# Token-major projections in a one-core hybrid attention block

## The chip, the core and the metric

The kernel runs on one core of a Trainium2 chip. The metric is device time: 1773.85 us, the median of 3 runs (1772.23 to 1774.06). TensorE multiplies, ScalarE (ACT) and VectorE (DVE) move, cast and combine, GpSimd (POOL) does a few side jobs, and SyncE (SP) issues nearly all transfers.

## The reference

One decoder block over 256 tokens of 2048 features, in float32, with weights of some 400 MB that are each read once.

```python
h = rmsnorm(x, norm_mix_g) * (1.0 + scale_m) + shift_m     # shift, scale, gate: silu(c) @ ada_w + ada_b
(p_q, p_k, p_v, p_g, p_gk, p_cq, p_ckv, p_kr, p_ga, p_gb) = split(h @ w_in)
o = gla_chunked(q, k, v, log_a)                            # gated linear attention, 4 heads
y_gla = (rmsnorm(o, gla_onorm_g) * silu(p_g)) @ gla_wo
y_mla = mla_attention(q_nope, q_rope, k_nope, k_rope, v_m) @ mla_wo      # 16 heads, causal softmax
merged = sigmoid(p_ga) * y_gla + sigmoid(p_gb) * y_mla
x = x + gate_m * (merged @ w_out)
h = rmsnorm(x, norm_ffn_g) * (1.0 + scale_f) + shift_f
g, u = split(h @ ffn_w_in)                                 # 2 x 5632 columns
x = x + gate_f * ((silu(g) * u) @ ffn_w_down)
out = rmsnorm(x, final_norm_g)
```

## The kernel before

Every product is made of three matmuls in the format fp32r. A weight piece `raw` of two k-tiles (2 x 128 rows) by 512 columns, 512 KB, is loaded by SyncE; ScalarE casts it to `hi` (L107), VectorE makes `lo = raw - hi` (L108), and TensorE adds hi x hi, hi x lo and lo x hi into PSUM. Such a piece is a *half* below, a *k-tile* is 128 of its rows. There are 6 raw buffers (up to 10 where spare slots are lent) and 3 each of `hi` and `lo`.

A group is 512 output columns over all 16 k-tiles and takes two PSUM banks (`mm`). It comes in two forms. `form_a` (L160) keeps a block of 128 tokens stationary and streams 512 weight columns: 6 matmuls for a k-tile, and the result lies token-major, 128 tokens by 512 features for each t. `form_b` (L170) keeps 128 weight columns stationary and streams 256 tokens: 12 matmuls for a k-tile, and the result lies feature-major, which is the form that a following projection needs as its activations.

The stages, in order: first projections of h in four rounds over its rows (jobs "a" and "b"; five of the eight branch gate groups are jobs 11 to 15), the low-rank attention (MLA) two heads at a time with the other three gate groups (`gate_stream`) and the linear attention's scores (GLA) between, GLA's output gate (`full(form_a, w_in, O_G ...)`), `mla_wo` gated, `gla_wo` with the merge, `w_out` with the residual, then the FFN: 11 chunks of a g group and a u group, and the down projection, whose 8 accumulators (2 token blocks by 4) take all PSUM banks.

The order of work: `tick()` runs after each half and moves what lies in the background, by paces (`pace`): the conditioning products (`ada_steps`), which load further 512 KB pieces and use VectorE, and two lanes of generators (`ATT`, two at a time, and `GLA`, one at a time); each `yield` there is a wait for the next tick. A scheduler then sets each engine's order by its own model of time.

In `mla_wo` and `gla_wo` the gates, which the first stages left in DRAM, come back as `mg` and `gaT` (`gate_in`, with the sigmoid); the group's PSUM result is multiplied by it, the two branches are added, and `mh`, `ml` are the merged tile's hi and lo for `w_out`. In the FFN, `sg` is silu of g, and the product of u and `sg` goes to `acts`; chunks 2 to 9 also turn two blocks of `x1` (the residual) over for the end, by four transposes (L884). A transpose is a TensorE matmul with an identity into an `aux` bank (2 of these), copied out by ScalarE.

Of the kernel before, what the change touches and what calls it, by code (L numbers as in the profile page):

```python
# [9 lines left out]
F32 = mybir.dt.float32  # L10
# [8 lines left out]
S = 256  # L19
P = 128  # L20
# [31 lines left out]
def tile_block(ctx: ExitStack, tc: tile.TileContext, x, positions, ada_w, ada_b, w_in, gla_gk_w, gla_wo,  # L52
# [18 lines left out]
    def k256(t):  # L71
        return t.rearrange("p (k t) -> p k t", t=S)
# [9 lines left out]

# [1 line left out]
    turn = [0]  # L84
# [95 lines left out]
    def group(form, w, c0, ah, al, nk, cols=512):  # L180
        ps = [mm_bank(), mm_bank()]
        for k in range(0, nk, 2):
            form(ps, half(w, k, c0, cols), ah, al, k, k == 0, k + 2 == nk, cols)
            yield ps
# [33 lines left out]

# [1 line left out]
    vec = const.tile([P, 164], F32, name="vec")  # L220
# [18 lines left out]

# [1 line left out]
    mod = const.tile([P, 96], F32, name="mod")  # L241
# [82 lines left out]

# [1 line left out]
    x_sp = dram.tile([P, 4096], F32, name="x_sp")  # L326
# [15 lines left out]

# [1 line left out]
    sin_t = const.tile([P, S], F32, name="sin_t")  # L344
# [31 lines left out]

# [1 line left out]
    latv = qk = vtv = None  # L378
# [30 lines left out]
    jobs += [("a", O_V + 512 * i, 512, vtv[:, :, 512 * i:512 * (i + 1)], None) for i in range(4)]  # L409
    jobs += [("b", o + 512 * i, 512, d, None) for (o, i), d in zip(gates, gdst)]  # L410
    NJ, PIN = len(jobs), 3
# [14 lines left out]
    for r in range(4):  # L426
# [38 lines left out]
        if r == 0:  # L465
# [3 lines left out]
            ang, ang2 = rope_angles()  # L469
# [1 line left out]
            pgk = const.tile([GR, S], F32, name="pgk")  # L471
# [3 lines left out]
            def latents():  # L475
# [10 lines left out]
                rsqrt_mean(rl, ssq, QR, 4)  # L486
                # rotary key on both halves of the partitions
                krd = sb(512, "sc", 2)[:, 0:S]
# [49 lines left out]

# [1 line left out]
    om = slot(5)  # L540
# [46 lines left out]
    def gate_stream():  # L587
        for o, i in gates[5:]:
            for ps in group(form_b, w_in, o + 512 * i, hhk, hlk, KT):
                yield  # L590
            st = raw_tile()
            for j in range(2):
                A.copy(out=st[:, 512 * j:512 * (j + 1)], in_=ps[j])
            G.dma_start(out=spill[o][:, 1024 * i:1024 * (i + 1)], in_=st)
# [44 lines left out]
    def gla_att(h):  # L639
# [9 lines left out]
        yield  # L649
        # log decay, times 16  # L650
        ps = gx_bank()
# [68 lines left out]

# [1 line left out]
    gt = slot(4)  # L722
# [53 lines left out]

# [1 line left out]
    oml = slot(1, F32R)  # L778
# [15 lines left out]
    for i in range(4):  # L794
        for n, ps in enumerate(group(form_b, mla_wo, 512 * i, k256(omh), k256(oml), KT)):
            tick()
            gate_in(mg, gb_sp, i, n)
        for j in range(2):
            d = mg[:, 1024 * i + 512 * j:1024 * i + 512 * (j + 1)]
            V.tensor_tensor(out=d, in0=ps[j], in1=d, op=ALU.mult)  # L800
    assert not GLA.busy()
    gaT = slot(3)
# [1 line left out]
    pace[0] = 0.65  # L804
    mh, ml = slot(2, F32R), slot(1, F32R)
    for i in range(4):
        for n, ps in enumerate(group(form_b, gla_wo, 512 * i, oghk, oglk, KT)):
            tick()
            gate_in(gaT, ga_sp, i, n)
        for j in range(2):  # L810
            cs = slice(1024 * i + 512 * j, 1024 * i + 512 * (j + 1))
            V.tensor_tensor(out=gaT[:, cs], in0=ps[j], in1=gaT[:, cs], op=ALU.mult)
            V.tensor_tensor(out=mg[:, cs], in0=mg[:, cs], in1=gaT[:, cs], op=ALU.add)
            A.copy(out=mh[:, cs], in_=mg[:, cs])
            V.tensor_tensor(out=ml[:, cs], in0=mg[:, cs], in1=mh[:, cs].bitcast(F32), op=ALU.subtract)

# [1 line left out]
    hold[0] = True  # L818
# [3 lines left out]
    for i in range(4):  # L822
# [7 lines left out]
        for j in range(4):  # L830
            k = 4 * i + j
            V.scalar_tensor_tensor(out=x1k[:, k], in0=ps[j // 2][:, (j % 2) * S:(j % 2 + 1) * S],
                                   scalar=mod[:, 32 + k:33 + k], in1=x1k[:, k], op0=ALU.mult, op1=ALU.add)
# [1 line left out]
    acc = sb(512, "w0")[:, :S]  # L835
# [29 lines left out]
    pace[0] = 0.5  # L865
    for ch in range(FFN // 512):
        if ch == 1:
            bg.append(slow())
        ps = full(form_b, ffn_w_in, 512 * ch, k256(fh), k256(fl), KT)
        sg = [sb(512, "w2"), sb(512, "w3")]  # L870
        for j in range(2):
            A.activation(out=sg[j], in_=ps[j], func=AF.Silu)
        ps = full(form_b, ffn_w_in, FFN + 512 * ch, k256(fh), k256(fl), KT)
        if ch == 8:
            acts[2] = slot(1)
        a = acts[ch // 4][:, (ch % 4) * 1024:(ch % 4 + 1) * 1024]
        for j in range(2):
            V.tensor_tensor(out=a[:, 512 * j:512 * (j + 1)], in0=ps[j], in1=sg[j], op=ALU.mult)
        if 2 <= ch < 10:
            k = 2 * (ch - 2)  # L880
            tp = aux_bank()
            for t in range(2):
                for kk in range(2):
                    T.transpose(out=tp[:, t * S + kk * P:t * S + (kk + 1) * P],  # L884
                                in_=x1k[:, k + kk, t * P:(t + 1) * P], identity=ident)
            A.copy(out=x1tv[:, :, k * P:(k + 2) * P], in_=tp.rearrange("p (t d) -> p t d", t=2))

    background(1000)
    acc = [[mm_bank() for _ in range(4)], [aux_bank(), aux_bank(), gx_bank(), gx_bank()]]
    NK, HELD = FFN // P, 4  # L890
# [7 lines left out]
    for k in range(NK):  # L898
# [10 lines left out]
        for hf in range(2):  # L909
            raw = load_raw(ffn_w_down[0, k * P:(k + 1) * P, hf * 1024:(hf + 1) * 1024], 1, 1024)  # L910
            if late:
                o = (k - NK + HELD) % 2 * 2048 + hf * 1024
                hi, lo = [u[:, o:o + 1024] for u in lh[(k - NK + HELD) // 2 * 2:][:2]]
                A.copy(out=hi, in_=raw[:, 0])
                V.tensor_tensor(out=lo, in0=raw[:, 0], in1=hi.bitcast(F32), op=ALU.subtract)
                ws.append((hi, lo))
                continue
            (hi, lo), = split_raw(raw, 1, 1024)
            for t in range(2):
                for n in range(2):  # L920
                    down(acc[t][2 * hf + n], ah, al, hi, lo, t, n, k == 0, False)
        if late:
            held.append((ah, al, ws))

# [1 line left out]
    ot = slot(4)  # L926
# [51 lines left out]
```

## Time and profile before

| | us |
|---|---|
| median of 3 runs | 1773.85 |
| span of the profiled execution | 1771.8 |
| TensorE busy | 1733.6 (98%) |
| VectorE busy | 1229.8 (69%) |
| ScalarE busy | 836.7 (47%) |
| DMA moved | 418.93 MB, mean 236 GB/s |

The profiled execution's own time is this span with what little lies around it; the runs' median is 2.05 us above the span. Busy times overlap between engines, and those of pipelined matmuls overlap among themselves, so the distance between two starts on TensorE tells more than a duration.

### The profile page before, as it was taken

To read this page: it belongs to the slowest core of one execution; us is meant where nothing else is said; L and a number is where in the kernel's file an instruction comes from. 1 tells how busy PE (TensorE), PEld (TensorE's weight loads), DVE (VectorE), ACT (ScalarE), POOL (GpSimd) and SP (SyncE) were. 2 spreads that over 40 slices of the span, in tenths; PEclk is the share of its full clock that TensorE was granted. 3 is DMA by queue.
4 is the path that set the end of the run, shared out by engine and by line. 5 is a ranking of instruction groups with operands and counts; after the bars stand their busy time and mean duration, and the time that the engine had idled before them with its cause. 6 is when DMAs were issued, how large, how long until landed. Compare 5 with 4: busy or idle time off the path is not lost. (4 is left out here: it accounts for less than half of the span.)

```text
span 1771.8 us, 31106 instructions
## 1 busy us (share of the span) xinstructions
PE 1733.6 (98%) x12416; PEld 1640.9 (93%) x12416; DVE 1229.8 (69%) x1764; ACT 836.7 (47%) x1278; POOL 96.9 (5%) x136
## 2 busy tenths in 40 slices
PE   6999999999999999999999999999999999999997
PEld 6899999899999988999999899999999999888885
DVE  7899887587777477888887856667564444455556
ACT  5544445356767655544444443333334333444443
POOL 1360000000000110000000000000000000000001
PEclk8999999999999999999999899999999999999999
DMA  9999886564445497999999567778775555555553
GB/s 359 322 325 303 283 308 216 181 204 150 152 136 178 134 329 253 350 356 329 332 321 305 203 201 257 244 227 267 234 226 181 182 185 179 179 191 191 191 189 106
DMA packets 207377, 418.93 MB, mean 236 GB/s; under 512 B 12960, under 2 KB 31840, under 8 KB 206592
## 3 DMA queue, kind: packets, MB, share of 16 engines
q1 hardware_dynamic: 205472, 410.39, 69.0%
q0 software_dynamic: 1616, 6.49, 1.0%
q8 instruction: 97, 1.59, 0.4%
q14 instruction: 48, 0.39, 0.1%
q10 hardware_dynamic: 144, 0.07, 0.0%
HBM read 408.51 MB, written 8.39 MB: 235 GB/s over the span
## 5 line engine op out<-in xcount | busy, mean ns | idle before, releaser
L108 DVE TENSOR_TENSOR lo<-raw,hi 128x1024 fp32r<-128x1024 f32 (+3 forms) x524 | 603.1, 1156 | 411.9 <-ACT hi L107 410.9
L176 PE MATMUL mm<-s,hi 128*128 128x256 f32 x3072 | 873.0, 285 | 2.5 <-ACT hi L107 2.1
L177 PE MATMUL mm<-s,hi 128*128 128x256 f32 x3072 | 869.2, 284 | 0.0
L178 PE MATMUL mm<-s,lo 128*128 128x256 f32 x3072 | 862.9, 284 | 2.0 <-DVE lo L108 2.0
L107 ACT CAST hi<-raw 128x1024 fp32r<-128x1024 f32 (+3 forms) x524 | 511.2, 982 | 676.7 <-PE mm L177 440.0
L176 PEld LDWEIGHTS mm<-s,hi 128*128 128x128 f32 x3072 | 590.5, 192 | 4.6 <-ACT hi L107 2.2
L177 PEld LDWEIGHTS mm<-s,hi 128*128 128x128 f32 x3072 | 590.8, 192 | 0.5 <-DVE s L781 0.2
L178 PEld LDWEIGHTS mm<-s,lo 128*128 128x128 f32 x3072 | 586.3, 192 | 3.6 <-DVE lo L108 2.7
L267 DVE SCALAR_TENSOR_TENSOR ada<-raw,cact,ada 128x512 f32<-128x512 f32 (+1 forms) x293 | 212.1, 728 | 7.9 <-DMA raw<-in_ada_w_dram 5.4
L107 ACT CAST hi<-s 128x1024 fp32r<-128x1024 f32 (+1 forms) x76 | 78.1, 1028 | 104.4 <-PE mm L177 62.2
L167 PE MATMUL mm<-lo,s 128*128 128x512 f32 (+1 forms) x320 | 123.9, 388 | 0.3 <-DVE lo L108 0.3
L168 PE MATMUL mm<-hi,s 128*128 128x512 f32 (+1 forms) x320 | 121.4, 382 | 1.7 <-DVE s L322 1.7
L166 PE MATMUL mm<-hi,s 128*128 128x512 f32 (+1 forms) x320 | 112.1, 386 | 0.9 <-ACT s L321 0.9
L108 DVE TENSOR_TENSOR lo<-s,hi 128x1024 fp32r<-128x1024 f32 (+1 forms) x76 | 91.4, 1203 | 29.7 <-ACT hi L107 29.4
L168 PEld LDWEIGHTS mm<-hi,s 128*128 128x128 f32 x320 | 60.7, 190 | 12.4 <-DVE s L322 2.0
L167 PEld LDWEIGHTS mm<-lo,s 128*128 128x128 f32 x320 | 60.7, 190 | 11.8 <-issue 0.8
L166 PEld LDWEIGHTS mm<-hi,s 128*128 128x128 f32 x320 | 60.2, 191 | 11.2 <-ACT s L321 1.2
L895 PE MATMUL mm<-lo,w 128*128 128x512 f32 x160 | 62.7, 392 | 0.0
L896 PE MATMUL mm<-hi,w 128*128 128x512 f32 x160 | 62.4, 392 | 0.0
L267 DVE SCALAR_TENSOR_TENSOR ada<-s,cact,ada 128x512 f32<-128x512 f32 (+1 forms) x79 | 57.7, 730 | 1.5 <-DMA s<-in_ada_w_dram 0.9
L894 PE MATMUL mm<-hi,w 128*128 128x512 f32 x160 | 50.4, 393 | 1.3 <-ACT w L902 1.3
L451 DVE TENSOR_TENSOR s<-mm,s 128x512 f32<-128x512 f32 (+1 forms) x62 | 40.5, 672 | 1.1 <-PE mm L178 0.7
(271 smaller groups left out, 1562.4 us busy)
## 6 DMA issues: line engine op xcount, KB each, us to landing
raw<-in_ffn_w_in_dram SPq DMA_DIRECT2D x176, 512.0 KB, 4.4
raw<-in_ada_w_dram SPq DMA_DIRECT2D x150, 512.0 KB, 5.0
raw<-in_w_in_dram SPq DMA_DIRECT2D x128, 512.0 KB, 4.6
raw<-in_ffn_w_down_dram SPq DMA_DIRECT2D x88, 512.0 KB, 4.5
s<-in_ada_w_dram SPq DMA_DIRECT2D x42, 512.0 KB, 5.8
s<-in_w_in_dram SPq DMA_DIRECT2D x32, 512.0 KB, 4.6
raw<-in_mla_wo_dram SPq DMA_DIRECT2D x20, 512.0 KB, 6.1
raw<-in_gla_wo_dram SPq DMA_DIRECT2D x20, 512.0 KB, 6.7
```

The lines of the kernel that those rows point to most:

```text
L107: A.copy(out=hh_, in_=rr)
L108: V.tensor_tensor(out=ll_, in0=rr, in1=hh_.bitcast(F32), op=ALU.subtract)
L166: T.matmul(ps[t][:, :cols], lhsT=ah[:, k, ts], rhs=hi, start=st, stop=False)
L167: T.matmul(ps[t][:, :cols], lhsT=ah[:, k, ts], rhs=lo, start=False, stop=False)
L168: T.matmul(ps[t][:, :cols], lhsT=al[:, k, ts], rhs=hi, start=False, stop=en)
L176: T.matmul(o, lhsT=hi[:, pick], rhs=ah[:, k], start=st, stop=False, skip_group_check=True)
L177: T.matmul(o, lhsT=hi[:, pick], rhs=al[:, k], start=False, stop=False, skip_group_check=True)
L178: T.matmul(o, lhsT=lo[:, pick], rhs=ah[:, k], start=False, stop=en, skip_group_check=True)
L267: ins = V.scalar_tensor_tensor(out=acc, in0=raw[:, k - k0], scalar=c, in1=acc, op0=ALU.mult, op1=ALU.add)
L894: T.matmul(o, lhsT=ah[:, ts], rhs=hi[:, ns], start=first, stop=False)
L895: T.matmul(o, lhsT=ah[:, ts], rhs=lo[:, ns], start=False, stop=False)
L896: T.matmul(o, lhsT=al[:, ts], rhs=hi[:, ns], start=False, stop=last)
```

## The change

Four projections go from `form_b` to `form_a`: the eight branch gate groups, `mla_wo`, `gla_wo` and the FFN's first projection. What lies in DRAM and in `mg` and `gaT` is then token-major, and so are the gating and the merge. Where the next projection wants features first, two generators in the lane `ATT` turn the result over: `turn_over` the merged tile (8 transposes for a group, then hi and lo from PSUM), `turn_act` the FFN's product (8 transposes for a chunk, then a copy to `acts`), both two ticks after the group. The `x1` transposes become a generator too (`turn_x1`). Before the down projection's first piece is done, the lane is emptied, and its second token block takes the `gx` banks first.

```diff
-    jobs += [("b", o + 512 * i, 512, d, None) for (o, i), d in zip(gates, gdst)]
+    jobs += [("a", o + 512 * i, 512, d.rearrange("p (t c) -> p t c", t=2), None) for (o, i), d in zip(gates, gdst)]
...
-            for ps in group(form_b, w_in, o + 512 * i, hhk, hlk, KT):
+            for ps in group(form_a, w_in, o + 512 * i, hhk, hlk, KT):
...
-        for n, ps in enumerate(group(form_b, mla_wo, 512 * i, k256(omh), k256(oml), KT)):
+        for n, ps in enumerate(group(form_a, mla_wo, 512 * i, k256(omh), k256(oml), KT)):
...
+    def turn_over(i):
+        yield
+        yield
+        for j in range(2):
+            ps = aux_bank()
+            for b in range(2):
+                for t in range(2):
+                    c0 = 1024 * i + 512 * t + (2 * j + b) * P
+                    T.transpose(out=ps[:, b * S + t * P:b * S + (t + 1) * P], in_=mg[:, c0:c0 + P], identity=ident)
+            cs = slice(1024 * i + 512 * j, 1024 * i + 512 * (j + 1))
+            A.copy(out=mh[:, cs], in_=ps)
+            V.tensor_tensor(out=ml[:, cs], in0=ps, in1=mh[:, cs].bitcast(F32), op=ALU.subtract)
+            yield
+
     for i in range(4):
-        for n, ps in enumerate(group(form_b, gla_wo, 512 * i, oghk, oglk, KT)):
+        for n, ps in enumerate(group(form_a, gla_wo, 512 * i, oghk, oglk, KT)):
...
-            A.copy(out=mh[:, cs], in_=mg[:, cs])
-            V.tensor_tensor(out=ml[:, cs], in0=mg[:, cs], in1=mh[:, cs].bitcast(F32), op=ALU.subtract)
+        ATT.wait.append(turn_over(i))
...
+    def turn_act(ch, sg):
+        yield
+        yield
         if ch == 8:
             acts[2] = slot(1)
         a = acts[ch // 4][:, (ch % 4) * 1024:(ch % 4 + 1) * 1024]
         for j in range(2):
-            V.tensor_tensor(out=a[:, 512 * j:512 * (j + 1)], in0=ps[j], in1=sg[j], op=ALU.mult)
+            tp = aux_bank()
+            for b in range(2):
+                for t in range(2):
+                    T.transpose(out=tp[:, b * S + t * P:b * S + (t + 1) * P],
+                                in_=sg[t][:, (2 * j + b) * P:(2 * j + b + 1) * P], identity=ident)
+            A.copy(out=a[:, 512 * j:512 * (j + 1)], in_=tp)
+            yield
...
-        ps = full(form_b, ffn_w_in, FFN + 512 * ch, k256(fh), k256(fl), KT)
+        ps = full(form_a, ffn_w_in, FFN + 512 * ch, k256(fh), k256(fl), KT)
+        for t in range(2):
+            V.tensor_tensor(out=sg[t], in0=ps[t], in1=sg[t], op=ALU.mult)
+        ATT.wait.append(turn_act(ch, sg))
         if 2 <= ch < 10:
...
+            ATT.wait.append(turn_x1(2 * (ch - 2)))
...
-    acc = [[mm_bank() for _ in range(4)], [aux_bank(), aux_bank(), gx_bank(), gx_bank()]]
+    acc = [[mm_bank() for _ in range(4)], [gx_bank(), gx_bank()]]
...
+            if k == 0 and hf == 1:
+                while ATT.busy():
+                    ATT.step()
+                acc[1] += [aux_bank(), aux_bank()]
```

How the instructions move is seen at three places. The first is TensorE in `gla_wo`, near the start of its second group; `s` is an activation tile (hi or lo part), `ada` a conditioning accumulator, the `s` of L815 the merged tile `mg`. Before:

```order
L176 MATMUL mm<-s_6934,hi 128x256
L177 MATMUL mm<-s_7617,hi 128x256
L178 MATMUL mm<-s_6934,lo 128x256
L176 MATMUL mm<-s_6934,hi 128x256
L289 MATMUL aux<-ident,ada 128x128 x4
L177 MATMUL mm<-s_7617,hi 128x256
```

And in the change:

```order
L166 MATMUL mm<-hi,s_5978 128x512
L167 MATMUL mm<-lo,s_5978 128x512
L168 MATMUL mm<-hi,s_5979 128x512
L166 MATMUL mm<-hi,s_5978 128x512 x2
L815 MATMUL aux<-ident,s_6859 128x128 x8
L167 MATMUL mm<-lo,s_5978 128x512
L168 MATMUL mm<-hi,s_5979 128x512
```

One matmul of 512 stands for two of 256, and the eight transposes of `turn_over` stand together, after 26 matmuls of the new group.

The second is VectorE at the end of `gla_wo`'s first group, where the products (L812, now L827), the sums (L813, now L828) and the lo parts (L815, now L818) are made. Before:

```order
L812 TENSOR_TENSOR s_8774<-mm,s_8774 128x512 x2
L267 SCALAR_TENSOR_TENSOR ada<-raw,cact,ada 128x512
L813 TENSOR_TENSOR s_7627<-s_7627,s_8774 128x512 x2
L108 TENSOR_TENSOR lo<-raw,hi 128x1024
L267 SCALAR_TENSOR_TENSOR ada<-raw,cact,ada 128x512
```

And in the change:

```order
L827 TENSOR_TENSOR s_7622<-mm,s_7622 128x512 x2
L267 SCALAR_TENSOR_TENSOR ada<-raw,cact,ada 128x512
L828 TENSOR_TENSOR s_6859<-s_6859,s_7622 128x512 x2
L108 TENSOR_TENSOR lo<-raw,hi 128x1024
L267 SCALAR_TENSOR_TENSOR ada<-raw,cact,ada 128x512
```

Products and sums stand as before; the lo parts move further back.

The third is TensorE where the FFN ends and the down projection begins; `w_16697` and `w_13207` are the hi and lo of its first activations, `w_13049` and `w_13050` the last chunk's products. Before:

```order
L178 MATMUL mm<-s_11034,lo 128x256
L176 MATMUL mm<-s_11034,hi 128x256
L177 MATMUL mm<-s_11035,hi 128x256
L178 MATMUL mm<-s_11034,lo 128x256
L894 MATMUL mm<-hi,w_16697 128x512
L895 MATMUL mm<-lo,w_16697 128x512
```

And in the change:

```order
L167 MATMUL mm<-lo,s_9538 128x512
L168 MATMUL mm<-hi,s_9539 128x512
L890 MATMUL aux<-ident,w_13049 128x128 x2
L890 MATMUL aux<-ident,w_13050 128x128
L890 MATMUL aux<-ident,w_13049 128x128
L890 MATMUL aux<-ident,w_13050 128x128 x2
L890 MATMUL aux<-ident,w_13049 128x128
L890 MATMUL aux<-ident,w_13050 128x128
L925 MATMUL mm<-hi,w_13207 128x512
```

The last chunk's eight transposes stand between, with no other matmul.

## Rows read from the trace of the kernel before

**Rows 1.** The page: busy time by engine; TensorE's granted clock in 40 slices.

```profile
PE 1733.6 (98%) x12416; PEld 1640.9 (93%) x12416; DVE 1229.8 (69%) x1764; ACT 836.7 (47%) x1278; POOL 96.9 (5%) x136
PEclk8999999999999999999999899999999999999999
```

**Rows 2.** TensorE's waits: engine, line, releaser, us in total, times, longest.

```profile
PE aux L213 <- DVE e L212: 4.0, 2, 3.0
...
PE mm L894 <- ACT w L902: 1.3, 1, 1.3
```

**Rows 3.** Groups by line and shape, TensorE: count, busy us, mean ns.

```profile
L176 PE MATMUL mm<-s,hi 128*128 128x256 f32 x3072 | 873.0, 285 | 2.5 <-ACT hi L107 2.1 <-ACT s L321 0.3
...
L166 PE MATMUL mm<-hi,s 128*128 128x512 f32 x256 | 92.3, 394 | 0.0
```

**Rows 4.** TensorE's timeline in the FFN: start us, duration us, line, tile, count.

```profile
1235.55 0.60 PE L884 MATMUL aux<-ident,s 128*128 128x128 f32 x4
1235.90 0.36 PE L176 MATMUL mm<-s,hi 128*128 128x256 f32 x1
1236.10 0.28 PE L177 MATMUL mm<-s,hi 128*128 128x256 f32 x1
...
1282.05 0.60 PE L884 MATMUL aux<-ident,s 128*128 128x128 f32 x4
```

**Rows 5.** TensorE's timeline in the output gate's projection, form a.

```profile
659.91 0.39 PE L166 MATMUL mm<-hi,s 128*128 128x512 f32 x1
660.14 0.39 PE L167 MATMUL mm<-lo,s 128*128 128x512 f32 x1
...
666.74 0.62 PE L166 MATMUL mm<-hi,s 128*128 128x512 f32 x2
```

**Rows 6.** ScalarE's timeline in the down projection: first and last of 32 casts.

```profile
1539.42 0.40 ACT L902 CAST w<-s 128x256 fp32r<-128x256 f32 x1
...
1710.30 0.40 ACT L902 CAST w<-s 128x256 fp32r<-128x256 f32 x1
```

**Rows 7.** TensorE's timeline at transposes between form a matmuls.

```profile
701.22 1.03 PE L751 MATMUL gx<-ident,s 128*128 128x128 f32 x8
702.00 0.48 PE L167 MATMUL mm<-lo,s 128*128 128x512 f32 x1
702.32 0.39 PE L168 MATMUL mm<-hi,s 128*128 128x512 f32 x1
```

**Rows 8.** Line L886, the copies from PSUM: ns min/median/max, first and last start.

```profile
L886 ACT COPY s<-aux x8: 567/579/587, 1003.0 to 1469.1; 128x512 f32<-128x512 f32 x8
```

**Rows 9.** VectorE's timeline at the end of `gla_wo`'s first group.

```profile
830.66 1.28 DVE L812 TENSOR_TENSOR s<-mm,s 128x512 f32<-128x512 f32 x2
...
832.52 1.28 DVE L813 TENSOR_TENSOR s<-s,s 128x512 f32<-128x512 f32 x2
```

**Rows 10.** Timeline of all engines where the down projection begins.

```profile
1514.04 1.46 DVE L878 TENSOR_TENSOR s<-mm,w 128x512 f32<-128x512 f32 x2
...
1514.49 0.28 PE L178 MATMUL mm<-s,lo 128*128 128x256 f32 x1
...
1515.65 0.71 ACT L902 CAST w<-s 128x256 fp32r<-128x256 f32 x2
...
1516.10 0.50 PE L894 MATMUL mm<-hi,w 128*128 128x512 f32 x1 [1.32 <-ACT w L902]
```

**Rows 11.** Stretches: us, busy PE, PEld, DVE, ACT, POOL, granted clock, DMA share, GB/s.

```profile
1003.00:1006.00 3.00, 2.89 (x13) 2.89 (x14) 2.96 (x8) 2.85 (x7) 0.00 (x0) 0.50 0.00 0
140.00:160.00 20.00, 20.00 (x167) 19.91 (x166) 20.00 (x33) 10.02 (x19) 0.00 (x0) 1.00 0.84 274
720.00:740.00 20.00, 19.96 (x167) 19.67 (x167) 16.35 (x23) 12.13 (x21) 2.29 (x12) 1.00 1.04 388
760.00:780.00 20.00, 20.00 (x169) 20.00 (x168) 17.23 (x22) 8.30 (x8) 0.00 (x0) 1.00 1.03 381
```

**Rows 12.** SyncE's waits between 700 and 800 us.

```profile
SPq L98 <- DVE lo L108: 44.7, 28, 4.1
```

More of the change, by code (lines that the diff above doesn't have):

```diff
@@ L865, in tile_block @@
     pace[0] = 0.5
[L866 to L872, printed above, removed]
-        ps = full(form_b, ffn_w_in, FFN + 512 * ch, k256(fh), k256(fl), KT)
+    def turn_act(ch, sg):
+        yield
+        yield
         if ch == 8:
@@ L877, in tile_block, with turn_x1 @@
         for j in range(2):
-            V.tensor_tensor(out=a[:, 512 * j:512 * (j + 1)], in0=ps[j], in1=sg[j], op=ALU.mult)
-        if 2 <= ch < 10:
[L880 to L886, printed above, removed]
+            tp = aux_bank()
[5 more added lines that the diff above has]
+            yield
+    def turn_x1(k):
+        tp = aux_bank()
+        for t in range(2):
+            for kk in range(2):
+                T.transpose(out=tp[:, t * S + kk * P:t * S + (kk + 1) * P],
+                            in_=x1k[:, k + kk, t * P:(t + 1) * P], identity=ident)
+        A.copy(out=x1tv[:, :, k * P:(k + 2) * P], in_=tp.rearrange("p (t d) -> p t d", t=2))
+        yield
+    assert not ATT.busy()
+    for ch in range(FFN // 512):
+        if ch == 1:
+            bg.append(slow())
+        ps = full(form_a, ffn_w_in, 512 * ch, k256(fh), k256(fl), KT)
+        sg = [sb(512, "w2"), sb(512, "w3")]
+        for t in range(2):
+            A.activation(out=sg[t], in_=ps[t], func=AF.Silu)
+        ps = full(form_a, ffn_w_in, FFN + 512 * ch, k256(fh), k256(fl), KT)
+        for t in range(2):
+            V.tensor_tensor(out=sg[t], in0=ps[t], in1=sg[t], op=ALU.mult)
+        ATT.wait.append(turn_act(ch, sg))
+        if 2 <= ch < 10:
+            ATT.wait.append(turn_x1(2 * (ch - 2)))
     background(1000)
-    acc = [[mm_bank() for _ in range(4)], [aux_bank(), aux_bank(), gx_bank(), gx_bank()]]
+    acc = [[mm_bank() for _ in range(4)], [gx_bank(), gx_bank()]]
     NK, HELD = FFN // P, 4
```

## The prediction

> **What bounds the kernel now.** I read the head of the page first: TensorE is busy for 98% of the span, and its granted clock is at the upper level (2.4 GHz) in every slice but the first, which shows 0.8 [rows 1]. A busy share of pipelined matmuls says little about how fast they go, so next come TensorE's own waits: after the first loads the longest are 4.0 us in two for `rows_of` (the row of inverse norms) and 1.3 us where the down projection starts [rows 2]. So TensorE's instruction stream is the bound: what counts is how far apart its instructions start, not how long one is under way (285 ns and 394 ns in the list by shape [rows 3], both mostly pipeline). The timeline gives the distances.
>
> Form b (a weight block stationary, 256 tokens moving): one chunk of the first FFN projection, from one set of four transposes to the next, takes 1282.05 - 1235.55 = 46.50 us for 2 groups x 16 k-tiles x 12 matmuls = 384 matmuls and the set [rows 4]. The set costs 1235.90 - 1235.55 = 0.35 us, and the first matmul behind it 0.20 instead of 0.12, together 0.43. (46.50 - 0.43) / 384 = 0.120 us per matmul of 256 columns.
>
> Form a (a token block stationary, 512 weight columns moving), in the output gate's projection: 30 matmuls from 659.91 to 666.74, so 6.83 / 30 = 0.2277 us [rows 5]. The down projection has the same shapes; there, 31 steps of 24 matmuls lie between two casts, (1710.30 - 1539.42) / 31 / 24 = 0.2297 us [rows 6]. Two matmuls of 256 take 0.240, one of 512 takes 0.228 to 0.230: each instruction carries some 13 ns besides its columns.
>
> **The change part by part.** *Matmuls.* 608 k-tiles of 512 output columns go from form b to form a: 80 in the first rounds (five gate jobs x 16), 48 in `gate_stream`, 64 in `mla_wo`, 64 in `gla_wo`, 352 in the FFN. Each removes 12 matmuls and adds 6. I take 0.228 per matmul: the new order has runs of three as in rows 5 and pairs of L166 as before the transposes, and rows 5 are the same code. 12 x 0.120 - 6 x 0.228 = 0.072 us; x 608 = 43.8 us saved. With rows 5 alone it is 0.074 and 44.8, with rows 6 0.062 and 37.6. TensorE has no cover here, so the time goes from the path unless something else becomes late.
>
> *Transposes.* 32 for the merged branches, 88 for the FFN's activations: 120. Among form a matmuls eight of them took 702.00 - 701.22 = 0.78 us, 0.0975 each, and the first matmul behind them 0.32 instead of 0.23, so 0.09 per set [rows 7]. The order cuts the 120 into 23 sets: 11.7 + 2.1 = 13.8 us. By rows 4 (0.43 per four) it would be 12.9; if each four stood alone by rows 7 (0.48) 14.4. The eight sets of `x1` transposes existed before; now they stand in 15 pieces (7 x 0.09 = 0.6), and two of the sets, which stood right behind `rows_of`, where TensorE waited 3.0 us at a time [rows 2], lose that cover (at most 8 x 0.11 = 0.9). Together 1.5.
>
> *Copies.* ScalarE gets 22 more copies from PSUM at about 0.58 us [rows 8], 12.8 us. ScalarE is busy for 47% of the span [rows 1]; these cost nothing unless a cast of `hi` is late for them, and in the FFN there are two such casts' worth of slack (three `hi` buffers). VectorE's operations stay the same in number and shape: the split of the merged tile reads PSUM now, the product reads the same.
>
> *The waits that are added.* Each set of transposes needs the finished product, and all that follows on TensorE queues behind it. In `gla_wo` the two products and the two sums end 832.52 + 1.28 - 830.66 = 3.1 us after the group [rows 9]; in the new order 26 matmuls, 5.9 us, stand between the group's end and the set. So these waits should be zero. At one place there is nothing between: where the FFN ends, eight transposes, a copy and a cast come in a chain before the first matmul of the down projection, because the cast writes the buffer that the transposes read. Before, that matmul came 1516.10 - 1514.49 = 1.61 us after the last one of the FFN, behind the second product (1514.04 + 1.46) and a cast [rows 10]. Now: products until about 1.9, transposes 0.87, copy 0.58, cast and start about 0.7, so 4.0: 2.4 more, of which 0.9 is in the transposes already. 1.5 us.
>
> The clock: after the 3.0 us wait before `rows_of` the granted clock stood at 0.50, the lower level, from 1003 to 1006 [rows 11]; after the 1.3 us wait at the down projection's start it did not fall [rows 1, 2]. The new waits there are about 2 us and then 1.2. If the clock falls, some 3 us at half speed cost 1.5 more.
>
> *What the faster stream runs into.* From 140 to 160 us VectorE is busy 20.00 of 20 us [rows 11]: in the first two rounds the conditioning work is level with TensorE, and I count the 15 halves of gate jobs there (30 k-tiles, 2.2 us) as not gained. In `mla_wo` the DMA engines are at a mean share of 1.03 to 1.04 with up to 388 GB/s [rows 11], yet SyncE mostly waits for buffers that VectorE has to free (44.7 us in that window [rows 12]), so transfers still run ahead; I count nothing there.
>
> Sum: -43.8 + 13.8 + 1.5 + 1.5 + 2.2 = -24.8 us. The profiled execution has a span of 1771.8 us, and the median of the runs is 2.05 above it, which I leave as it is: 1773.85 - 24.8 = 1749.
>
> The Trainium skill speaks against the change at this point. Its page "TensorE: Matmul & The Clock Gate" (section "Back-to-back issue gap") has an isolated gap of N / 2.4 + 2.5 ns at full clock, 109 ns for 256 columns and 216 for 512, so that what an instruction costs beyond its columns is small. By that a k-tile would save 0.016 us, 608 of them 9.5, and 120 transposes would cost 6.7 (56 ns each): an estimate of 2.8 us gained, too little to be seen. This case's rows 4 to 6 show 120 and 228 to 230 ns instead.
>
> **The rivals.** 0.2% of the time, 3.5 us, is about what a measurement of this kernel can tell from no change.
>
> *The cover ends: 1758.* The data or VectorE become the bound in `mla_wo` and `gla_wo`, whose 128 k-tiles (9.2 us) then gain nothing: 24.8 - 9.2 = 15.6. For it: the DMA share above 1 in rows 11. Against: rows 12, and that the `hi` and `lo` buffers let TensorE run two halves ahead.
>
> *The instruction's own cost isn't saved: 1774, no change.* If the converted stages ran at 0.235 us per matmul, each k-tile would save 0.030 us, 18 in all, just what the additions cost (13.8 + 1.5 + 1.5). Against: all form a rows lie at 0.2277 to 0.2297, with the same code. It is also where the rule of the Trainium skill would end.
>
> *TensorE waits at its own transposes: slower, 1785.* The place is the first set behind each group in `gla_wo` and the FFN, 14 of them (4 and 10). If VectorE finishes the product late, TensorE stands, since the set comes in order before the next group's matmuls. It decides against the change from (24.8 + 3.5) / 14 = 2.0 us of wait at each, that is products 7.9 us after the group's end; at 2.6 us it would be 1749 + 36 = 1785. For it: VectorE has `lo` and conditioning work queued between. Against: 3.1 us in rows 9, and an emptier VectorE in the FFN.
>
> **How the numbers follow.** My forecast, 1749, gets 0.76; the ended cover 0.16; no change 0.04; slower 0.04. The likeliest case's own range is 1742 (44.8 saved, 12.9 for the transposes, nothing lost at the rounds or the clock: 30 us, and 2 us for the spread of the runs) to 1757 (37.6 saved, 14.4 for the transposes, the clock's 1.5: 16.5). The range for 8 in 10 reaches into the ended cover: 1742 to 1760. Faster by over 0.2%: 0.92, within it 0.04, slower 0.04.
>
> **What would show it.** In the profile after: L166 to L168 at 0.228 apart through the FFN, and a chunk (2 x 96 matmuls with 8 or 12 transposes) in 44.7 to 45.3 us against 46.50. No TensorE wait at the transposes of L815 and L890 but at the last chunk, and about 4 us from the last FFN matmul to the first of L925. ACT and VectorE with the same busy time but for 12.8 us on ACT. I am wrong if L166 to L168 come at 0.235 or more, if `hi` waits for a DMA in `mla_wo`, or if the waits on VectorE before L815 and L890 sum to over 10 us.

## The result

The changed kernel takes 1747.92 us (median of 4 runs, 1746.09 to 1749.22) against 1773.45 (4 runs, 1772.23 to 1774.06): a ratio of 0.9855, 95% interval 0.9841 to 0.9869. The profiled executions' spans are 1771.8 and 1747.1 us, 24.7 apart; the forecast's sum was 24.8.

The head of the page after, the rows that answer to [rows 1]:

```profile
PE 1705.2 (98%) x8888; PEld 1461.1 (84%) x8888; DVE 1226.6 (70%) x1764; ACT 847.6 (49%) x1300; POOL 99.7 (6%) x136
PEclk8999999999999999999999899999999999999998
```

TensorE is as full as before, with 3528 instructions fewer (608 x 6 = 3648 matmuls less, 120 transposes more). VectorE has the same 1764 operations, and ScalarE is busy for 10.9 us more (12.8 were forecast). The clock row has an 8 at the 23rd slice in both kernels, and in the one after a further one at the end.

TensorE's groups by shape after, which answer to [rows 3] (form a has taken over):

```profile
L167 PE MATMUL mm<-lo,s 128*128 128x512 f32 x1456 | 576.8, 396 | 2.0 <-DVE lo L108 1.9
L176 PE MATMUL mm<-s,hi 128*128 128x256 f32 x672 | 191.7, 286 | 0.0
```

TensorE's waits after (in us: total, times, longest), against [rows 2]:

```profile
PE aux L213 <- DVE e L212: 4.2, 2, 3.0
...
PE aux L576 <- ACT sc L571: 2.2, 1, 2.2
...
PE mm L925 <- ACT w L933: 0.7, 1, 0.7
...
PE aux L890 <- DVE w L914: 0.4, 2, 0.3
```

L213 is as long as it was. L890, the FFN's new transposes, wait 0.4 us in all; L815, the merged tile's, have no row. New is the second row: softmax transposes of the attention that wait for ScalarE.

Where the time went is read from the last start of the operation that ends each stage. First five lines of before (line, duration min/median/max in ns, first and last start in us):

```profile
L451 DVE TENSOR_TENSOR s<-mm,s x62: 530/681/693, 113.1 to 391.1; 128x512 f32<-128x512 f32 x58, 128x368 f32<-128x368 f32 x4
...
L771 ACT COPY s<-mm x8: 576/588/590, 635.1 to 710.0; 128x512 f32<-128x512 f32 x8
...
L800 DVE TENSOR_TENSOR s<-mm,s x8: 680/684/693, 738.2 to 807.4; 128x512 f32<-128x512 f32 x8
...
L812 DVE TENSOR_TENSOR s<-mm,s x8: 678/682/692, 830.7 to 901.2; 128x512 f32<-128x512 f32 x8
...
L878 DVE TENSOR_TENSOR s<-mm,w x22: 676/681/692, 1051.0 to 1514.8; 128x512 f32<-128x512 f32 x22
```

And the same operations after (L812 has become L827, L878 has become L914):

```profile
L451 DVE TENSOR_TENSOR s<-mm,s x62: 530/682/692, 113.6 to 388.2; 128x512 f32<-128x512 f32 x58, 128x368 f32<-128x368 f32 x4
...
L771 ACT COPY s<-mm x8: 586/589/593, 630.6 to 705.7; 128x512 f32<-128x512 f32 x8
...
L800 DVE TENSOR_TENSOR s<-mm,s x8: 679/687/692, 733.9 to 799.2; 128x512 f32<-128x512 f32 x8
...
L827 DVE TENSOR_TENSOR s<-mm,s x8: 678/682/685, 821.6 to 891.2; 128x512 f32<-128x512 f32 x8
...
L914 DVE TENSOR_TENSOR w<-mm,w x22: 675/681/685, 1039.7 to 1488.8; 128x512 f32<-128x512 f32 x22
```

| up to | before | after | difference so far | this stage |
|---|---|---|---|---|
| first rounds, L451 last | 391.1 | 388.2 | -2.9 | -2.9 |
| attention and output gate, L771 last | 710.0 | 705.7 | -4.3 | -1.4 |
| `mla_wo`, L800 last | 807.4 | 799.2 | -8.2 | -3.9 |
| `gla_wo`, L812 / L827 last | 901.2 | 891.2 | -10.0 | -1.8 |
| `w_out` and first FFN chunk, L878 / L914 first | 1051.0 | 1039.7 | -11.3 | -1.3 |
| ten more FFN chunks, L878 / L914 last | 1514.8 | 1488.8 | -26.0 | -14.7 |
| the rest of the span | 1771.8 | 1747.1 | -24.7 | +1.3 |

A chunk went from (1514.8 - 1051.0) / 10 = 46.4 us to (1488.8 - 1039.7) / 10 = 44.9.

Each trace is one execution, and the first rows are good to some 2 us only: by the same lines the kernels of the experiments below that share the change's code up to there end the first rounds at 386.5 to 388.3, and e3, which shares the code of before, at 390.1. The ten chunks repeat better: 449.1 in the changed kernel, e3 and e6.

Where the FFN ends, the timeline of all engines after (start, duration, engine; in brackets the idle time before), against [rows 10]:

```profile
1488.20 1.28 DVE L914 TENSOR_TENSOR w<-mm,w 128x512 f32<-128x512 f32 x2
1488.27 0.39 PE L168 MATMUL mm<-hi,s 128*128 128x512 f32 x1
...
1488.94 0.44 PE L890 MATMUL aux<-ident,w 128*128 128x128 f32 x2 [0.28 <-DVE w L914]
...
1489.54 0.87 PE L890 MATMUL aux<-ident,w 128*128 128x128 f32 x6 [0.16 <-DVE w L914]
...
1490.12 0.59 ACT L892 COPY s<-aux 128x512 f32<-128x512 f32 x1 [0.38 <-PE aux L890]
1490.60 0.41 ACT L933 CAST w<-s 128x256 fp32r<-128x256 f32 x1
...
1491.06 0.50 PE L925 MATMUL mm<-hi,w 128*128 128x512 f32 x1 [0.65 <-ACT w L933]
```

The chain is the one forecast: product, transposes, copy, cast, first matmul. From the last FFN matmul (1488.27) to the first of the down projection (1491.06) it takes 2.79 us, where 4.0 was forecast. The copy needs four of the eight transposes and begins (1490.12) while others still run (1489.54 + 0.87), so part of them lies beside it.

Where the FFN begins, TensorE's timeline after:

```profile
990.61 1.22 PE L213 MATMUL aux<-e,ones 128*128 128x256 f32 x2 [2.99 <-DVE e L212]
993.01 0.79 PE L166 MATMUL mm<-hi,s 128*128 128x512 f32 x1 [1.18 <-ACT s L321]
993.60 0.63 PE L167 MATMUL mm<-lo,s 128*128 128x512 f32 x1
994.03 0.63 PE L166 MATMUL mm<-hi,s 128*128 128x512 f32 x1
```

Its matmuls come 0.43 us apart, not 0.228. Two stretches of after, there and behind the L576 wait (us, busy PE, PEld, DVE, ACT, POOL, granted clock, DMA share, GB/s), show why:

```profile
993.00:996.00 3.00, 2.99 (x7) 2.41 (x8) 3.00 (x9) 2.06 (x5) 0.00 (x0) 0.50 0.00 0
...
606.00:609.00 3.00, 2.86 (x10) 1.73 (x9) 1.78 (x5) 2.83 (x6) 0.38 (x2) 0.62 0.26 100
```

The granted clock is 0.50 there, the lower level of 1.2 GHz, and mixed (0.62) behind the L576 wait.

### The profile page after: what moved, and what is told of

Same layout as the page of the kernel before. It is cut to its first block, busy times and chain, and to the rows that moved or that the text cites. A ratio compares the mean times of both kernels' runs of the same rounds, so it can differ in the third digit from the quotient of the medians.

```text
span 1747.1 us, 24089 instructions
## 1 busy us (share of the span) xinstructions
PE 1705.2 (98%) x8888; PEld 1461.1 (84%) x8888; DVE 1226.6 (70%) x1764; ACT 847.6 (49%) x1300; POOL 99.7 (6%) x136
## 5 line engine op out<-in xcount | busy, mean ns | idle before, releaser
L108 DVE TENSOR_TENSOR lo<-raw,hi 128x1024 fp32r<-128x1024 f32 (+3 forms) x524 | 600.9, 1152 | 396.9 <-ACT hi L107 394.4
L107 ACT CAST hi<-raw 128x1024 fp32r<-128x1024 f32 (+3 forms) x524 | 512.4, 984 | 620.6 <-PE mm L168 391.1
L167 PE MATMUL mm<-lo,s 128*128 128x512 f32 (+1 forms) x1520 | 598.4, 394 | 2.6 <-DVE lo L108 2.6
L168 PE MATMUL mm<-hi,s 128*128 128x512 f32 (+1 forms) x1520 | 590.4, 390 | 1.7 <-DVE s L322 1.7
L166 PE MATMUL mm<-hi,s 128*128 128x512 f32 (+1 forms) x1520 | 543.2, 393 | 4.3 <-ACT hi L107 2.1
L166 PEld LDWEIGHTS mm<-hi,s 128*128 128x128 f32 x1520 | 286.7, 190 | 63.3 <-ACT s L321 3.1
L167 PEld LDWEIGHTS mm<-lo,s 128*128 128x128 f32 x1520 | 287.8, 189 | 61.4 <-DVE lo L108 5.2
L168 PEld LDWEIGHTS mm<-hi,s 128*128 128x128 f32 x1520 | 287.3, 189 | 58.7 <-DVE s L322 2.0
L176 PE MATMUL mm<-s,hi 128*128 128x256 f32 x672 | 191.7, 286 | 0.0
L177 PE MATMUL mm<-s,hi 128*128 128x256 f32 x672 | 190.1, 284 | 0.0
L178 PE MATMUL mm<-s,lo 128*128 128x256 f32 x672 | 188.3, 284 | 0.0
L176 PEld LDWEIGHTS mm<-s,hi 128*128 128x128 f32 x672 | 128.7, 192 | 0.8 <-issue 0.3
L177 PEld LDWEIGHTS mm<-s,hi 128*128 128x128 f32 x672 | 128.8, 192 | 0.4
L178 PEld LDWEIGHTS mm<-s,lo 128*128 128x128 f32 x672 | 127.5, 192 | 0.0
L108 DVE TENSOR_TENSOR lo<-s,hi 128x1024 fp32r<-128x1024 f32 (+1 forms) x76 | 91.7, 1207 | 27.1 <-ACT hi L107 26.5
L451 DVE TENSOR_TENSOR s<-mm,s 128x512 f32<-128x512 f32 (+1 forms) x62 | 40.1, 672 | 0.2
```

The lines of the kernel that those rows point to most:

```text
L107: A.copy(out=hh_, in_=rr)
L108: V.tensor_tensor(out=ll_, in0=rr, in1=hh_.bitcast(F32), op=ALU.subtract)
L166: T.matmul(ps[t][:, :cols], lhsT=ah[:, k, ts], rhs=hi, start=st, stop=False)
L167: T.matmul(ps[t][:, :cols], lhsT=ah[:, k, ts], rhs=lo, start=False, stop=False)
L168: T.matmul(ps[t][:, :cols], lhsT=al[:, k, ts], rhs=hi, start=False, stop=en)
L176: T.matmul(o, lhsT=hi[:, pick], rhs=ah[:, k], start=st, stop=False, skip_group_check=True)
```

## The experiments

The kernels of the first four were timed on one chip (before: 1773.69 us), those of the next three on one (1773.63), the last two on one (1772.67), so about 1 us between kernels of different chips says nothing.

**Transposes left out (e1).** The transposes of both new generators are replaced by copies of the untransposed data, so the projections behind them compute on wrongly ordered activations:

```diff
-            tp = aux_bank()
-            for b in range(2):
-                for t in range(2):
-                    T.transpose(out=tp[:, b * S + t * P:b * S + (t + 1) * P],
-                                in_=sg[t][:, (2 * j + b) * P:(2 * j + b + 1) * P], identity=ident)
-            A.copy(out=a[:, 512 * j:512 * (j + 1)], in_=tp)
+            A.copy(out=a[:, 512 * j:512 * (j + 1)], in_=sg[j])
```

> The changed kernel with the 120 added transposes left out: hi and lo of the merged tile and the FFN's product are copied as they lie, token-major, so the following projections compute on wrongly ordered data; all copies, products and waits stay. Theory (the transposes lie open on TensorE at 0.0975 us each and 0.09 per set): 13.8 us less than the changed kernel and about 1 more where the FFN ends, so 1733. Rival (they partly stand in time that TensorE would have lost anyway, and the matmuls gained less than reckoned): 1740 to 1748.

Measured: 1733.54 us (1732.25 to 1734.31), ratio 0.9773 [0.9758, 0.9787]. By the medians, leaving them out is worth 1747.92 - 1733.54 = 14.4 us, where 13.8 and about 1 more at the down projection were expected, and without them the saving is 1773.45 - 1733.54 = 39.9. But more changed than the 120 transposes, so 14.4 is not their price. e1's `x1` transposes, its FFN products, TensorE's start of the down projection, and a stretch behind it:

```profile
L889 PE MATMUL aux<-ident,s x32: 270/272/421, 985.8 to 1032.9; 128*128 128x128 f32 x32
...
L904 DVE TENSOR_TENSOR w<-mm,w x22: 678/681/686, 1035.2 to 1470.8; 128x512 f32<-128x512 f32 x22
...
1473.13 0.50 PE L915 MATMUL mm<-hi,w 128*128 128x512 f32 x1 [2.48 <-ACT w L923]
...
1474.00:1477.00 3.00, 3.00 (x8) 2.32 (x8) 0.00 (x0) 0.00 (x0) 0.00 (x0) 0.50 0.48 176
```

All 32 `x1` transposes moved ahead of the ten chunks; in the changed kernel they lie among them. The down projection starts no sooner: its first matmul comes 2.87 us after the last of the FFN (1470.26), against 2.79, since product, copy and cast still form a chain. TensorE waits 2.48 us in one piece there, the granted clock behind it is 0.50, and the rest of the span is 259.7 us, 1.4 longer than in the change.

Single stages give cleaner prices. The ten chunks of e1 hold no transposes at all: (1470.8 - 1035.2) / 1920 = 0.2269 us per matmul. Before, with six sets of `x1` transposes among them, it is (463.8 - 6 x 0.43) / 3840 = 0.1201. So a k-tile saves 12 x 0.1201 - 6 x 0.2269 = 0.080 us, the 320 of the ten chunks 25.6. In `gla_wo` the 24 transposes of three groups cost 92.0 - 89.3 = 2.7 us (e1's L800 ends at 797.0 and its `gla_wo` product at 886.3).

**Form b with 128 tokens at a time (e2).** Each matmul of `w_out`, which stays in form b, is split in two of 128 tokens with the same weight block, 768 becoming 1536:

```diff
-        for n, ps in enumerate(group(form_b, w_out, 512 * i, k256(mh), k256(ml), KT)):
+        for n, ps in enumerate(group(form_c, w_out, 512 * i, k256(mh), k256(ml), KT)):
...
+                    for t in range(2):
+                        c = (b % 2) * S + t * P
+                        T.matmul(ps[b // 2][:, c:c + P], lhsT=wt[:, pick], rhs=x[:, k, t * P:(t + 1) * P],
...
```

> The changed kernel with the output projection w_out (still form b) cut finer: each matmul of 256 tokens becomes two of 128 with the same stationary weights, 1536 matmuls for each group... in all 4 x 16 x 24 = 1536 instead of 768, the same columns. Theory (a fixed 13 ns per instruction beside its columns): 67 ns per matmul, 1536 x 0.067 - 768 x 0.120 = +10.7 us, so 1759. Rival 1 (form b is bound by loading 128 weight columns for each matmul, so 0.120 whatever moves): 1536 x 0.120 - 92 = +92 us, 1840. Rival 2 (columns alone count): within 2 us of the changed kernel, 1748 to 1750.

Measured: 1825.23 us (1824.28 to 1826.09), ratio 1.029 [1.0275, 1.0306], 77.3 above the change. TensorE's timeline in it:

```profile
919.97 0.39 PE L188 MATMUL mm<-s,lo 128*128 128x128 f32 x2
920.19 0.50 PE L188 MATMUL mm<-s,hi 128*128 128x128 f32 x3
```

Two instructions start in 920.19 - 919.97 = 0.22 us, 0.110 each; over the 18 from 921.72 to 923.73 it is 0.112. 768 of 0.120 are 92.2 us; (92.2 + 77.3) / 1536 = 0.110 as well. Half the columns save about 0.010 us of 0.120. A constant of 13 ns beside the columns would give 0.066 here: this theory falls. With 128 stationary columns these instructions take about 0.110 us even for half the moving columns.

**The FFN alone (e3), the branches alone (e4).** The two halves of the change, each put on the kernel before:

```diff
-            for ps in group(form_a, w_in, o + 512 * i, hhk, hlk, KT):
+            for ps in group(form_b, w_in, o + 512 * i, hhk, hlk, KT):
...
-        for n, ps in enumerate(group(form_a, mla_wo, 512 * i, k256(omh), k256(oml), KT)):
+        for n, ps in enumerate(group(form_b, mla_wo, 512 * i, k256(omh), k256(oml), KT)):
```

(the core of e3 against the changed kernel; `gla_wo` and the first rounds go back likewise; e4 is the same for `ffn_w_in`).

> The kernel before with only the FFN's first projection in form a and its products turned over. Theory (each part is worth its own matmuls less its own transposes): by the two traces the FFN gained 1.9 us in its first chunk and 14.7 in the ten others and lost 1.0 at the down projection's start: 15.6 less than before, so 1758. Rival (one common cause, as a program of fewer instructions or another schedule): either nearly the whole 25.5 us or far less than 15.

> The changed kernel with the FFN as before: gates, mla_wo and gla_wo in form a, the merged tile turned over. Theory: the two traces stand 9.4 us apart at the end of w_out, so 9 to 10 less than before: 1764, and with the FFN's alone the sum is the whole change. Rival (the data or VectorE hold these stages, so that the gain there is spread by chance of the schedule): 1767 to 1773.

Measured: 1758.59 us for the FFN alone, ratio 0.9917 [0.9902, 0.9932], 15.1 gained; 1762.58 for the branches alone, ratio 0.9934 [0.9918, 0.9951], 11.1 gained. Together 26.2, against 25.5 for the whole: the halves add. What was expected of both was read from the traces before and after, so this doesn't test the prediction's prices. TensorE's wait at L576, in e4's answer:

```profile
PE aux L576 <- ACT sc L571: 2.2, 1, 2.2
```

It is there in e4 and e1 and has no row in e3 or before, so it belongs to the branch half.

**Fewer stationary columns (e5).** `w_out` again in form b, its four groups with 128 tokens moving and 64 or 32 weight columns stationary, then 256 tokens and 64 or 32; most of its output is left out, and the time means nothing:

```diff
+    SHAPES = ((64, P), (32, P), (64, S), (32, S))
...
+                        T.matmul(ps[b // 2][:m, c:c + n], lhsT=wt[:, b * P:b * P + m], rhs=x[:, k, t * n:(t + 1) * n],
...
```

> The changed kernel with w_out in form b cut to four shapes, one for each of its groups, the first k-tile whole: 128 moving columns with 64 and with 32 stationary columns, 256 moving with 64 and with 32; most of w_out's output is left out. It asks what the 0.110 us of the cut to 128 tokens is, and what the 13 ns above 256 columns are. Theory (loading 128 stationary columns takes 0.110 and is a floor; beside it stands a fixed 13 ns per instruction): 0.067 us per matmul in the first two groups, 0.120 in the last two. Rival 1 (0.110 is the least distance of any load and matmul): 0.110 in the first two, 0.120 in the last two. Rival 2 (the 13 ns come from the load too): 0.055 to 0.067 in the first two, 0.107 to 0.113 in the last two.

Measured, TensorE's timeline with 64 stationary and 128 moving, then with 32 and 256:

```profile
892.10 0.40 PE L191 MATMUL mm<-s,hi 128*64 128x128 f32 x4
892.34 0.28 PE L191 MATMUL mm<-s,lo 128*64 128x128 f32 x2
892.46 0.40 PE L191 MATMUL mm<-s,hi 128*64 128x128 f32 x4
...
967.60 0.39 PE L191 MATMUL mm<-s,hi 128*32 128x256 f32 x2
967.83 0.28 PE L191 MATMUL mm<-s,lo 128*32 128x256 f32 x1
967.94 0.39 PE L191 MATMUL mm<-s,hi 128*32 128x256 f32 x2
```

Six instructions in 892.46 - 892.10 = 0.36 us, 0.060 each; three in 0.34, 0.113 each. The other two groups (32 and 128; 64 and 256) have the same distances. So with half the stationary columns the floor of 0.110 is gone, and at 256 moving columns 0.120 becomes 0.113, as the second rival had it. 128 more moving columns take 0.113 - 0.060 = 0.053 us, so 256 take 0.106 of the 0.120. Of the other 14 ns some 7 stay with 64 or 32 stationary columns, and some 7 come with 128; whether by their load or by the width of the result is not shown. The Trainium skill ("TensorE: Matmul & The Clock Gate", section "LDWEIGHTS (loading the stationary operand)") gives a load P / 1.2 ns, 107 for 128 columns and 53 for 64; the 110 measured with 128 lie just above the first. It isn't a floor for all: the transposes, which also load 128 columns, in f32, come 0.0975 us apart in [rows 7].

**The down projection's first buffer (e6).** Its first cast writes a buffer that the last transposes don't read:

```diff
-        aa = sb(512, ("w2", "w3", "w0", "w1")[k % 4], 1, F32R)
+        aa = sb(512, ("w0", "w1", "w2", "w3")[k % 4], 1, F32R)
```

> The changed kernel, but the down projection's first activations go to buffers w0 and w1 and not to w2 and w3, which the last chunk's transposes still read. Theory (the start of the down projection waits for the chain of transposes, copy and cast): TensorE goes from the last FFN matmul to the first of the down projection in about 0.3 us, where it took 2.79 with 0.87 of transposes in it; the transposes come later in the stream, so 1.6 to 1.7 us less: span 1745.4, median 1746. Rival (the chain is late anyway and TensorE waits for it a little further on): no change, 1747 to 1748.

Measured: 1746.05 us (1744.71 to 1747.01), ratio 0.9843 [0.983, 0.9857]. By times alone that isn't told from the change; TensorE's timeline tells it:

```profile
1487.57 0.39 PE L168 MATMUL mm<-hi,s 128*128 128x512 f32 x1
1487.80 0.61 PE L925 MATMUL mm<-hi,w 128*128 128x512 f32 x2
...
1491.45 0.82 PE L890 MATMUL aux<-ident,w 128*128 128x128 f32 x6
```

The down projection starts 0.23 us after the last FFN matmul, and the transposes stand among its own. The chain of 2.79 us came from the shared buffer.

**The gap at the FFN's start filled (e7).** e6, and all 32 `x1` transposes put ahead of `rows_of`, where TensorE waits, in the `gx` banks, and not among the FFN's matmuls:

```diff
+    for k in range(0, KT, 2):
+        tp = gx_bank()
+        for t in range(2):
+            for kk in range(2):
+                T.transpose(out=tp[:, t * S + kk * P:t * S + (kk + 1) * P],
+                            in_=x1k[:, k + kk, t * P:(t + 1) * P], identity=ident)
+        A.copy(out=x1tv[:, :, k * P:(k + 2) * P], in_=tp.rearrange("p (t d) -> p t d", t=2))
...
-            ATT.wait.append(turn_x1(2 * (ch - 2)))
```

> As the one before, and the 32 transposes of the residual x1 are taken from the FFN's chunks (where they cost 0.0975 us each and 0.09 for each of 15 pieces, 4.5 us) and put ahead of the norm, where TensorE waits 3.0 us for the inverse norms and 1.2 for the first activations, in the banks gx. Theory: 4.5 us less, and up to 1 more if the granted clock no longer falls there: 1740 to 1742. Rival (the eight copies that ScalarE makes for them, 4.6 us, hold up the modulation, which then starts the FFN later by what was gained): 1745 to 1747.

Measured: 1738.77 us (1738.3 to 1739.99), ratio 0.9806 [0.9792, 0.9819]: faster than both kernels, 9.2 us under the change and a little under what was expected. TensorE's timeline and a stretch of it there:

```profile
987.58 1.15 PE L866 MATMUL gx<-ident,s 128*128 128x128 f32 x8 [0.19 <-ACT s L868]
989.35 0.70 PE L213 MATMUL aux<-e,ones 128*128 128x256 f32 x2 [0.62 <-DVE e L212]
991.23 0.50 PE L166 MATMUL mm<-hi,s 128*128 128x512 f32 x1 [1.18 <-ACT s L321]
991.56 0.40 PE L167 MATMUL mm<-lo,s 128*128 128x512 f32 x1
```

```profile
992.00:995.00 3.00, 3.00 (x14) 2.44 (x13) 3.00 (x9) 2.09 (x4) 0.00 (x0) 1.00 0.00 0
```

The wait of 2.99 is 0.62, and the granted clock stays at 1.00. In the change some 14 matmuls came 0.43 apart (993.01 to 999.15, clock 0.50 to 999), 14 x 0.20 = 2.8 us. L912, the FFN's product, gives the rest:

```profile
L912 DVE TENSOR_TENSOR w<-mm,w x22: 677/681/684, 1035.0 to 1480.0; 128x512 f32<-128x512 f32 x22
```

The ten chunks take 1480.0 - 1035.0 = 445.0 us instead of 449.1: 4.1 for the `x1` sets that no longer stand among them (by the prediction's prices 32 x 0.0975 + 15 x 0.09 = 4.5). With e6's start of the down projection, 1.9 us by the medians, these are 8.8 of the 9.2. Against e1's ten chunks, which have no transposes, the 80 of the FFN's products cost 445.0 - 435.6 = 9.4 us here.

**One more tick before the softmax transposes (e8, e9).** In the changed kernel and in e7, for all heads of the attention:

```diff
             A.activation(out=sc[:, sl], in_=sc[:, sl], func=AF.Copy, scale=st[:, 4 + i:5 + i])
         yield
         yield
+        yield
         ps = aux_bank()
```

> The changed kernel with one more tick of the lane between the softmax's last scaling on ScalarE (L571) and the transposes of the probabilities (L576), for all heads. In the changed kernel TensorE waits 2.2 us there once (at 605.4), and the granted clock is 0.62 and 0.82 in the six us behind it. Theory (the wait is a matter of how many matmuls stand between, and costs itself and the clock behind it): no wait at L576, the clock stays at 1.00, and 2 to 4 us less than the changed kernel: 1744 to 1746. Rival (ScalarE has more queued than the stream covers at this place, so the work only ends later): the wait moves to the next step of the lane (L581 or L583) or to the end of the attention, and the time stays at 1747 to 1749.

> e7_gap_fill with the same extra tick. By the theory of e8 the two gains stand in different places and add: 1735 to 1737. By the rival 1738 to 1740, as e7.

Measured: 1746.24 us (1745.52 to 1748.53), ratio 0.9851 [0.9835, 0.9867], and 1740.0 (1738.97 to 1740.92), ratio 0.9817 [0.9802, 0.9832]. Neither differs from its parent by what can be told. TensorE's timeline of e8 at the place:

```profile
599.70 0.58 PE L167 MATMUL mm<-lo,s 128*128 128x512 f32 x1
...
601.94 0.39 PE L168 MATMUL mm<-hi,s 128*128 128x512 f32 x1
602.17 0.49 PE L577 MATMUL aux<-ident,sc 128*128 128x128 f32 x3
604.82 0.33 PE L577 MATMUL aux<-ident,sc 128*128 128x128 f32 x1 [2.16 <-ACT sc L571]
...
606.15 1.22 PE L166 MATMUL mm<-hi,s 128*128 128x512 f32 x2
```

The wait is as long as it was, and the same ten L166 to L168 stand ahead of the transposes (599.70 to 601.94; in the changed kernel 600.25 to 602.49): at this place, the end of the attention, the extra tick came without matmuls. So the runs show that a tick doesn't help, not which theory is right. ScalarE is busy 3.00 of 3.00 us from 603 to 606 in e8 and in the changed kernel, which speaks for the rival; more matmuls at this place, or less work for ScalarE, were not tried, and why the kernel before has no wait here stays open.

## Why the prediction was right

The forecast, 1749, is 1 us from 1747.92, by the mechanism it named: TensorE's stream is shorter and hardly anything else became late. The mechanism is shown best in the FFN's ten chunks, where leaving parts out one by one splits the 14.7 us gained there: the matmuls save 25.6 (before against e1; 23.0 by the forecast's price), 80 transposes cost 9.4 (e7 against e1; 9.2 at 13.8 / 120 each), and the `x1` sets 4.1 - 2.6 = 1.5 more (e7, and 6 x 0.43 before; 1.5 forecast). That the whole came out within 1 us is in part luck: by these sizes a larger gain from the matmuls made up for waits and a lower clock elsewhere that the forecast had not priced.

- *Matmuls, 43.8 us.* Too small where it can be seen alone: 0.080 us for a k-tile in the FFN's ten chunks and not 0.072, so 25.6 us where 23.0 was priced; in the other stages the price wasn't measured by itself. Its reason was wrong in part: "each instruction carries some 13 ns besides its columns". e2 and e5 show that about half of it comes with 128 stationary columns, which also keep these matmuls some 0.110 us apart at the least that was measured. Form a has half as many instructions, and so half as many loads, for the same columns streamed, and so pays both halves of the 13 ns half as often.
- *Transposes, 13.8 us.* Held: 2.7 us for 24 in `gla_wo` and 9.4 for 80 in the FFN are 0.116 each; 13.8 / 120 is 0.115. e1's 14.4 lies near it by chance, as its `x1` sets moved and its clock fell.
- *`mla_wo`.* 4.6 forecast, 3.9 gained. [Rows 11]'s DMA share is the same after (1.02 and 1.04 in the same stretches) with up to 399 GB/s, and no wait for a DMA: the data of the rival "the cover ends" didn't come in. Its VectorE came near: TensorE waited for `lo` (L108) twice, 0.6 us together, which it didn't in this stage before, and VectorE's 16.35 us of [rows 11] became 19.86 in this stretch:

```profile
720.00:740.00 20.00, 19.39 (x88) 15.58 (x88) 19.86 (x28) 13.07 (x22) 0.00 (x0) 1.00 1.02 383
```

- *`gla_wo`.* 4.6 less its three sets of transposes (2.6) is 2.0; 1.8 gained.
- *First rounds.* 5.8 - 2.2 = 3.6 forecast, 2.9 gained (1.8 to 4.6 by the other traces). That the first two gain nothing agrees with the trace (VectorE is busy for 19.98 of 20 us from 140 to 160 us after, and the last product of the second round was evacuated at 153.09 before and 153.84 after), but was not tested.
- *Waits at the transposes.* None at L815 and 0.4 us at L890, both at the FFN's end, as forecast. The slower rival, 2 us at each of 14 places, had nothing: the products were done while the next group's matmuls ran.
- *The down projection's start.* 4.0 forecast, 2.79 measured, since the cast needs only the first copy, and that only four transposes. e6 shows that the shared buffer was the cause.
- *Not forecast: the wait at L576.* In the attention, 2.2 us, and the clock at 0.62 behind it. The stage up to the output gate's end gained 1.4 (up to 3.0 by the other traces), where 48 k-tiles x 0.072 = 3.5 were forecast.
- *The clock.* The prediction said that it is at the upper level in every slice but the first. The row shown as [rows 1] has a second 8, where the FFN begins, and was misread. What was priced (1.5 us at the down projection) didn't come: the waits there are 0.28, 0.16 and 0.65, with transposes between. The risk was real, for in e1 one wait of 2.48 us at this place was followed by three us at 0.50. What came was not priced: with the two `x1` sets gone from behind `rows_of`, the form a matmuls started at 993.01, 2.4 us behind L213, and ran at the lower level to 999; e7 shows 2.8 us of it. Not all of this is new, since the kernel before was at 0.50 there from 1003 to 1006 ([rows 11]).
- *The rule of the Trainium skill* ("TensorE: Matmul & The Clock Gate", section "Back-to-back issue gap"), by which the prediction reckoned 2.8 us gained, doesn't hold for these pairs of load and matmul: with 256 moving columns its isolated gap is 109 ns and the row 120; nearest is 113, with 64 or 32 stationary columns. The section has that gap for a single matmul and says that in a stream of such pairs both set the spacing, so the prediction took it further than it goes. (By the formula a k-tile saves 6 x 2.5 ns = 0.015 us, not 0.016, and the estimate is 2.4.)

## What to carry to other kernels

Where TensorE's stream is the bound and each matmul loads its own stationary block, take as stationary the side that lets each load serve more moving columns, and price it by the measured distance of starts at both shapes, with the transposes that it makes necessary. Before work is moved off TensorE's waiting places, look at what it did there: it can have been free, and the time at the lower clock can be shorter with it (from the FFN's first matmul, 6.1 us in the changed kernel, and 3.4 before, with two `x1` sets there). Here putting transposes into such a gap gave 7 us more. At the seam of two stages see which buffer the first write of the second shares with the last read of the first.

## What was not expected of the hardware

- fp32r matmuls with 128 stationary columns came 0.110 to 0.112 us apart even with 128 moving columns; with 64 or 32 stationary it was 0.060, and 0.113 for 256 moving (0.120 with 128).
- After a wait of 2.99 us, 1.22 us of matmuls and another 1.18 of waiting, the granted clock stood at 0.50 for some 6 us of work; with sets of eight transposes ahead, and waits of 0.62 and 1.18 us, it stayed at 1.00 (e7). After the 2.2 us wait at L576 it was 0.62 over three us (0.50 in e8), and after 2.48 us of waiting in e1 0.50 over three.
- A loss of a few us is hard to see in the page's clock row: the slice of 43.7 us with the L576 wait reads 9. The stretches show it.
